# A hybrid MoBA/NSA decoder layer: k's norm weights applied behind the transposition, mixer B's gates finished in one piece, and a pair's first doubling put behind its subtraction

## The chip, the cores and the metric

The kernel runs on one core of a Trainium2 chip. Its five engines are named as in the profile: PE (matrix products), DVE (vector), ACT (scalar), POOL (GpSimd) and SP (issues most DMAs). Each has its own stream of instructions and runs it in order; they wait for each other through semaphores. The metric is the device time of one execution in microseconds (us), as a median of several runs.

## The reference

One decoder layer on x of 1 x 512 x 1024, all in float32. One input projection feeds two attention mixers of 8 heads with 64 channels each; their outputs are gated, projected, merged and projected once more. Cut to what the change touches:

```
h = rms_norm(x, norm_w);  proj = h @ w_in
q_a, k_a, v_a, z_a, q_b, kc, vc, ksl, vsl, kwn, vwn, gate_b, z_b, gate_m = split(proj)
o_a = moba_mixer(rms_norm(q_a, q_norm_a), rms_norm(k_a, k_norm_a), v_a, bias_a)
k_cmp = rms_norm(compress(kc), k_norm_cmp);  v_cmp = compress(vc)
o_b = nsa_mixer(rms_norm(q_b, q_norm_b), k_cmp, v_cmp,
                rms_norm(ksl, k_norm_sel), vsl, rms_norm(kwn, k_norm_win), vwn, gate_b, bias_b)
# in nsa_mixer: g = sigmoid(gate_b);  o = g0 * o_cmp + g1 * o_sel + g2 * o_win
y = sigmoid(gate_m) * (o_a*silu(z_a) @ w_branch_a) + ... (o_b*silu(z_b) @ w_branch_b)
x = x + y @ w_out
```

`rms_norm(k, g)` divides each head's 64 values by their root mean square and multiplies them by the 64 weights g. These weights are the same for all tokens. Since q and k only meet in the product q.k, the kernel multiplies the weights of q into those of k, with the factor 1/8 of the logits, and never touches q with them.

## The kernel before

**Products.** Each float32 product is made as three products of high and low parts (`mm3`, L386): a value is rounded to fp32r (its high part, a CAST) and the rest is a second fp32r tile (its low part, a subtraction). For weights, `wh` is made by ACT (L352), or now and then by POOL (L356) or DVE, and `wl = wr - wh` by DVE (L361, also for `vl`), now and then by POOL.

**Projections by token.** `proj_norm` runs over four tiles of 128 tokens for `qk0` and `qk1` (mixer A: four heads of q and four of k in 512 columns each) and for `kb` (mixer B: two groups of k_sel and of k_win, 256 columns, and 24 gate columns behind them). PE accumulates a tile into PSUM (`pgt`). Then `norm` (L709) makes a chain of steps: ACT copies the tile with the token's factor (L718) and squares it (L720), DVE sums per head (L721), DVE and POOL make the factors `nr` (L426, L427), DVE or POOL multiplies (L723). The last step multiplies k by its weights: for `qk` the second half of the columns (L726, 128x256, eight of them), for `kb` all columns (L729, 128x256, four of them). `gi` says which weights: 1 for mixer A's k, 4 and 5 for k_sel and k_win, 0 for none.

**Gates of mixer B.** With each tile of `kb`, ACT writes exp(-x) of the 24 gate columns into `ge` (L745), and at the end of the chain DVE adds 1 (L749) and writes the reciprocals into `gate[:, :, t]` (L750). `gate` is a 128x96 tile, read much later, when POOL scales the exponentials of mixer B's heads (L1062).

**Pairs of heads.** `k_pair` (L969) makes the k operands of two heads. PE transposes four 128x128 pieces into a PSUM bank (`pq`, L947, pool of three banks "t"). From its halves r = 0, 1 (64 partitions each) ACT writes the high part twice, into the lower and upper 64 partitions of `ks` (L978: four copies of 64x512 a pair), DVE subtracts to make the low part `kx` (L980, two a pair; the second frees the bank), and ACT doubles `kx` into its own upper 64 partitions (L983, two a pair). So a pair's chain is four copies, two subtractions, two doublings. PE's scores are `ks` by `qs` (L1024) and `kx` by `qs` (L1025), into `sps`. There are six pairs: four of mixer A and two of mixer B; the latter two also copy their first 128 columns into `kf` (L987).

**Around them.** `compress` makes mixer B's compressed keys: X differences and `xs` (L838, L706, L707), products `hps` (L862), `hs` (L868), their transposition `pu` (L873), then a chain of ACT and DVE on `gt` (L878 to L882), of which L882 frees the bank of `pu`. The softmax of a block of scores is DVE's L1043 (add the bias, take the row's maximum), ACT's L1058 (exponential and sum), DVE's L1061 (reciprocal), POOL's L1062 (scale); then PE transposes (`pt`, L1071), ACT and DVE split it into `ph` (L1083) and `pl` (L1085), and PE multiplies by v (`O`, L1105). `vb` (L768, L769) is mixer B's v.

**What sets the order.** A planner in Python runs while the program is built. Steps are put into a `Chain` with a cost for each engine that may do them (`c.do({"A": 478}, ...)`); a heap always takes the chain with the smallest time, gives its step to the engine on which the costs end it first, and advances that engine's planned time. PE's work is a set of generators that yield their costs. The order in which the planner emits is the order in which each engine runs. A step keeps its planned cost even if its function emits nothing.

**Constants.** `load_consts` (L1547) loads the constants tile `cst` in two parts (the identity first, the rest by the DMA at its end) and the gains `gn`, 6 x 64 numbers repeated on all partitions. DVE multiplies q's weights and 1/8 into k's (L1560, four products of 128x64).

## Time and profile before

| what | value |
|---|---|
| median of 3 runs | 452.53 us (452.14 to 452.53) |
| the profiled execution | 451.59 us |
| its span in the trace | 449.8 us |
| instructions | 8544 |
| clock granted to PE | 1.0 of full speed throughout |
| HBM traffic | 282 GB/s over the span |

Busy times are sums over the span and say nothing on where an engine is late. They are read by stretches, and together with PE's waits. A row of the timeline gives the start in us, the length in us, the engine, the line, the operation, what it writes and reads, shape and type, and how many such instructions follow each other; in brackets stands how long the engine stood idle before it, and what released it. A PE matmul's rows overlap: PE's rate is read from one start to the next. For instance, DVE's and ACT's groups with the most busy time are the low and high parts of the weights:

```profile
L361 DVE TENSOR_TENSOR wl<-wr,wh 128x512 fp32r<-128x512 f32 (+1 forms) x150 | 102.6, 701 | 2.1 <-ACT wh L352 1.8
L352 ACT CAST wh<-wr 128x512 fp32r<-128x512 f32 (+1 forms) x130 | 77.0, 608 | 15.3 <-DMA wr<-wsum 6.5
```

### The profile page before, as it was taken

The numbers are of one execution on the slowest core, as the hardware profiler recorded it, in microseconds if no ns is written. First come the engines' busy times: TensorE is split into PE (matmuls) and PEld (weight loads), VectorE is DVE, ScalarE is ACT, GpSimd is POOL, SyncE is SP. The second block draws the span as 40 slices with busy tenths as digits, with TensorE's granted clock in tenths as the row PEclk, the third lists the DMA queues.
The fourth block names the chain that finished last, engine by engine and source line by source line (L and its number), as shares of the span: only waits on it lengthen the run. The fifth ranks groups of instructions, "written<-read, shape, count | busy, mean of one in ns | idle before, by whom it ended". The sixth has DMA issues, their size and how long they took to land.

```text
span 449.8 us, 8544 instructions
## 1 busy us (share of the span) xinstructions
PE 441.8 (98%) x2779; PEld 394.0 (88%) x2779; DVE 384.0 (85%) x943; ACT 302.9 (67%) x711; POOL 198.9 (44%) x235
## 2 busy tenths in 40 slices
PE   8999999999999999999999999999999999999997
PEld 7878888899778899888999998989988999998886
DVE  5999899899998797788899899977967699899783
ACT  6866778867978798376878677687764355454450
POOL 1153337865675573177675654764850222211000
PEclk9999999999999999999999999999999999999999
DMA  8975746887975879858978876986767878789872
GB/s 262 305 253 187 242 150 213 196 228 187 267 181 165 214 220 270 290 142 202 287 213 204 228 181 170 253 218 156 213 166 174 256 220 253 223 245 290 278 237 95
DMA packets 55086, 98.21 MB, mean 218 GB/s; under 512 B 5313, under 2 KB 9537, under 8 KB 55041
## 3 DMA queue, kind: packets, MB, share of 16 engines
q1 hardware_dynamic: 39808, 68.30, 47.2%
q0 software_dynamic: 7616, 14.68, 20.4%
q10 hardware_dynamic: 7616, 14.68, 9.7%
q8 instruction: 22, 0.36, 0.3%
q14 instruction: 24, 0.19, 0.1%
HBM read 90.69 MB, written 36.31 MB: 282 GB/s over the span
## 4 chain that ended last, share of the span: by engine, by line
PE 77%; DVE 12%; ACT 4%; issue 3%; DMA 2%; POOL 0%; SPq 0%; DVEq 0%; ACTq 0%
PE pgw L386 18%; PE pgt L386 14%; PE pbr L386 9%; PE po L386 9%; PE pgc L386 7%; PE O L1105 6%; PE pt L1071 5%; PE sps L1024 3%; PE sps L1025 3%; DVE wl L361 2%; DMA wr<-in_wgate 2%; DVE sb L1043 1%; DVE pl L1085 1%; DVE sq L490 1%; PE pq L947 1%
## 5 line engine op out<-in xcount | busy, mean ns | idle before, releaser
L361 DVE TENSOR_TENSOR wl<-wr,wh 128x512 fp32r<-128x512 f32 (+1 forms) x150 | 102.6, 701 | 2.1 <-ACT wh L352 1.8
L352 ACT CAST wh<-wr 128x512 fp32r<-128x512 f32 (+1 forms) x130 | 77.0, 608 | 15.3 <-DMA wr<-wsum 6.5
L356 POOL TENSOR_SCALAR wh<-wr 128x512 fp32r<-128x512 f32 (+1 forms) x39 | 31.6, 822 | 76.4 <-DVE wl L361 34.4
L1062 POOL TENSOR_SCALAR P<-P,sst,gate 128x512 f32<-128x512 f32 (+3 forms) x56 | 46.2, 828 | 40.0 <-DVE sst L1061 32.0
L1058 ACT ACTIVATE P<-sb,sst 128x512 f32<-128x512 f32 (+3 forms) x88 | 50.7, 577 | 17.5 <-DVE sst L1043 16.0
L1043 DVE CUSTOM_DVE_ANT_0 sb<-sps,T 128x512 f32<-128x512 f32 (+3 forms) x96 | 46.0, 483 | 14.0 <-PE sps L1025 13.5
L386 PE MATMUL pgt<-wh,hh 128*128 128x512 f32 (+2 forms) x160 | 56.6, 354 | 0.0
L386 PE MATMUL pgt<-wl,hh 128*128 128x512 f32 (+2 forms) x160 | 55.8, 349 | 0.8 <-DVE wl L361 0.8
L386 PE MATMUL pgt<-wh,hl 128*128 128x512 f32 (+2 forms) x160 | 55.7, 348 | 0.0
L386 PE MATMUL pgw<-th,wh 128*128 128x256 f32 x240 | 48.9, 281 | 0.3 <-DVE gm L1519 0.3
L1083 ACT CAST ph<-pt 128x512 fp32r<-128x512 f32 (+2 forms) x72 | 33.8, 476 | 19.8 <-PE pt L1071 18.5
L386 PE MATMUL pgw<-hh,wh 128*128 128x256 f32 x160 | 45.1, 282 | 0.5 <-ACT c L1460 0.5
L386 PE MATMUL pgw<-hl,wh 128*128 128x256 f32 x160 | 44.3, 277 | 0.0
L386 PE MATMUL pgw<-hh,wl 128*128 128x256 f32 x160 | 44.3, 277 | 0.0
L1071 PE MATMUL pt<-cst,P 128*128 128x128 f32 x232 | 40.7, 272 | 0.3 <-DVE pl L1085 0.3
L1085 DVE TENSOR_TENSOR pl<-pt,ph 128x512 fp32r<-128x512 f32 (+2 forms) x72 | 38.7, 549 | 1.8 <-ACT ph L1083 1.5
L386 PEld LDWEIGHTS pgw<-th,wh 128*128 128x128 f32 x240 | 39.4, 188 | 0.8 <-DVE gm L1519 0.5
L427 POOL TENSOR_TENSOR nr<-nss,mhalf 128x8 f32<-128x8 f32 (+1 forms) x16 | 26.4, 1650 | 22.5 <-DVE nss L426 19.3
L386 PEld LDWEIGHTS pgt<-wl,hh 128*128 128x128 f32 x160 | 30.0, 188 | 5.2 <-DVE wl L361 1.2
L386 PE MATMUL pgw<-th,wl 128*128 128x256 f32 x120 | 33.3, 277 | 0.0
L386 PEld LDWEIGHTS pgt<-wh,hh 128*128 128x128 f32 x160 | 30.1, 188 | 3.4 <-ACT nraw L718 0.2
L386 PEld LDWEIGHTS pgt<-wh,hl 128*128 128x128 f32 x160 | 30.1, 188 | 3.3
(271 smaller groups left out, 1289.4 us busy)
## 6 DMA issues: line engine op xcount, KB each, us to landing
wr<-wsum SPq DMA_DIRECT2D x56, 256.0 KB, 3.8
wr<-in_wtok SPq DMA_DIRECT2D x36, 256.0 KB, 4.8
wsum<-in_wgate ACTq DMA_DIRECT2D x16, 512.0 KB, 5.2
wsum<-wsum POOLq DMA_DIRECT2D x14, 512.0 KB, 7.6
wr<-in_wgate SPq DMA_DIRECT2D x24, 256.0 KB, 5.0
xsum<-th SPq DMA_DIRECT2D x16, 256.0 KB, 2.3
T<-rtab SPq DMA_DIRECT2D x16, 256.0 KB, 5.3
wr<-in_w SPq DMA_DIRECT2D x16, 256.0 KB, 4.3
```

The costliest lines, as they stand in the source:

```text
L352: e.copy(hi, raw)
L356: e.tensor_scalar(hi, raw, 1.0, 1.0, op0=ALU.mult, op1=ALU.mult)
L361: c.do({"D": cd(n)} if lead else either(n), lambda e, hi=hi, lo=lo, raw=raw: e.tensor_sub(lo, raw, hi.bitcast(F32))).mark((w, 1, i))
L386: nc.tensor.matmul(dst, sts[i][a], mvs[i][b], start=(start and i == a == b == 0), stop=(stop and i == n - 1 and b == 1), skip_group_check= ...
L427: c.do({"p": 430 + POWC * w}, lambda e: e.tensor_tensor(v(dst), v(ss), mhalf[:parts, :w], op=ALU.pow))
L1043: e.tensor_tensor_reduce(z["sb"][:, :L], sps[:, :L], T[:, S - L:], scale=-1.0, scalar=3e38, op0=ALU.add, op1=ALU.min, accum_out=st[:, 0, b ...
L1058: e.activation(pv(), z["sb"][:, :L], AF.Exp, bias=st[:, 0, b:b + 1], scale=-1.0, accum_out=st[:, 1, b:b + 1])
L1062: c.do({"P": 315 + 0.834 * L}, lambda e: e.tensor_scalar(pv(), pv(), st[:, 2, b:b + 1], g, op0=ALU.mult, op1=ALU.mult))
L1071: nc.tensor.transpose(pt[:, (b - kb) * P:(b - kb + 1) * P], u.p0 if u.p0 is not None and b == 0 else u.pb[:, POFF[b] + kb * P:POFF[b] + (k ...
L1083: e.copy(z["w"][0], pt[:, :w])
L1085: ch.do({"D": cd(w)}, lambda e: e.tensor_sub(z["w"][1], pt[:, :w], z["w"][0].bitcast(F32)), pt)
L1105: nc.tensor.matmul(O[0][:, S - n:], v.bitcast(F32) if kb == 3 else v, w, start=(u.first and kb == 0 and i == 0), stop=(u.last and kb == 3 ...
```

## The change

1. **k's weights behind the transposition.** `norm` no longer multiplies by the weights of k (L726, L729); the planner still counts the steps' costs, so that it gives the other work the same order. In `k_pair` a channel of k is a partition, so the weights are one column of factors, `gcol`: the four ACT copies become activations with that column as their scale, and the two subtractions become `pt * gcol - ks`, one DVE instruction each.
2. **Where the column comes from.** The six gains stand as six more columns in the second part of the constants (`cst` grows from 128x486 to 128x492). Three of the four products with q's weights (mixer A's k, k_sel, k_win) are made there, 128x1 each; the fourth (for the compressed k) stays as it was.
3. **The gates finished once.** ACT writes exp(-x) straight into `gate[:, :, t]`; the addition and the reciprocal are left out for the first three tiles and done for all 96 columns with the fourth.
4. **The first doubling.** The doubling of the pair's first `kx` gets a chain of its own, due 600 ns behind the planned end of its subtraction, instead of standing behind the second subtraction.

```diff
--- before.py
+++ after.py
@@ -29,7 +29,7 @@
 C32 = 32
 CMPH = 256
 COFF, NCST = {}, 0
-for _n, _w in (("ident", P), ("ii", DH), ("cmask", NT * C32), ("rowv", NT), ("hmask", 2), ("pos", 32), ("w2", 256)):
+for _n, _w in (("ident", P), ("ii", DH), ("cmask", NT * C32), ("rowv", NT), ("hmask", 2), ("gcol", 6), ("pos", 32), ("w2", 256)):
     COFF[_n] = (NCST, _w)
     NCST += _w
 POFF = [0, 128, 384, 768]
@@ -55,6 +55,7 @@
 LAND = 1000
 SLOW = dict(D=1.01, A=1.01, P=1.05)
 POWC = 180
+KX0 = 600
 CMARGIN = 1000
 UNITS = 4
 W1B = 2
@@ -414,6 +415,7 @@
         return cst[:, o:o + n]
 
     ident = cview("ident")
+    gcol = cview("gcol")
     ii = cview("ii")
     cmask = cview("cmask").rearrange("p (b c) -> p b c", b=NT)
     rowv = cview("rowv")
@@ -722,11 +724,9 @@
         rsqrt_mean(ch, lambda: b["r"], lambda: b["ss"], DH, H)
         ch.do(either(n), lambda e: e.tensor_mul(out, b["raw"], b["r"].unsqueeze(2).to_broadcast([P, H, DH])), lambda: b["t"])
         if gi == 1:
-            z = out[:, 4:]
-            ch.do(either(256), lambda e: e.tensor_mul(z, z, gn[:, 1, :].unsqueeze(1).to_broadcast([P, 4, DH])))
+            ch.do(either(256), lambda e: None)
         elif gi:
-            z = out.rearrange("p (a b) d -> p a b d", a=2)
-            ch.do(either(256), lambda e: e.tensor_mul(z, z, gn[:, gi:gi + 2, :].unsqueeze(2).to_broadcast([P, 2, 2, DH])))
+            ch.do(either(256), lambda e: None)
 
     def hl4(t):
         return t.rearrange("p (h s d) -> p h s d", s=2, d=DH)
@@ -741,13 +741,13 @@
             toks[name][t] = att(name, F32)
             ch = Chain(now[0] + 230)
             if name == "kb":
-                e_ = sp.tile([P, 24], F32, name=nm("ge"), tag="ge", bufs=4)
-                ch.do({"A": 164}, lambda e: e.activation(e_, ps[:, 256:280], AF.Exp, scale=nrx[:, t:t + 1]))
+                ch.do({"A": 164}, lambda e: e.activation(gate[:, :, t], ps[:, 256:280], AF.Exp, scale=nrx[:, t:t + 1]))
             norm(ch, toks[name][t], ps, t, 4 if name == "kb" else 8, gi)
             if name == "kb":
                 def g1(e):
-                    e.tensor_scalar_add(e_, e_, 1.0)
-                    e.reciprocal(gate[:, :, t], e_)
+                    if t == NT - 1:
+                        e.tensor_scalar_add(gate, gate, 1.0)
+                        e.reciprocal(gate, gate)
                 ch.do({"D": 300}, g1)
             ch.mark(f"{name}.{t}")
         yield from gemm_tok(name, emit, tags)
@@ -966,21 +966,28 @@
                  pt if r else None)
             box.append((z, c))
 
-    def k_pair(boxes, name, col, firsts=None):
+    def k_pair(boxes, name, col, gi, firsts=None):
 
         yield room("t")
         pt = turn(name, col)
         yield 4 * 109
         c = Chain(now[0] + 230)
         kk = [(att("ks"), att("kx")) for _ in range(2)]
+
+        def double():
+            nc.scalar.copy(kk[0][1][64:128, :], kk[0][1][0:64, :].bitcast(F32))
         for r, (ks, kx) in enumerate(kk):
             for i in range(2):
-                c.do({"A": 478}, lambda e, r=r, z=ks[64 * i:64 * i + 64, :]: e.copy(z, pt[64 * r:64 * r + 64, :]))
+                c.do({"A": 478}, lambda e, r=r, z=ks[64 * i:64 * i + 64, :]: e.activation(
+                    z, pt[64 * r:64 * r + 64, :], AF.Copy, scale=gcol[64 * r:64 * r + 64, gi:gi + 1]))
         for r, (ks, kx) in enumerate(kk):
-            c.do({"D": 602}, lambda e, r=r, ks=ks, kx=kx: e.tensor_sub(
-                kx[0:64, :], pt[64 * r:64 * r + 64, :], ks[0:64, :].bitcast(F32)), pt if r else None)
+            c.do({"D": 602}, lambda e, r=r, ks=ks, kx=kx: e.scalar_tensor_tensor(
+                kx[0:64, :], pt[64 * r:64 * r + 64, :], gcol[64 * r:64 * r + 64, gi:gi + 1], ks[0:64, :].bitcast(F32),
+                op0=ALU.mult, op1=ALU.subtract), pt if r else None)
+            if not r:
+                c.call(lambda: Chain(c.t + KX0).call(double))
         for r, (ks, kx) in enumerate(kk):
-            c.do({"A": ca(512)}, lambda e, kx=kx: e.copy(kx[64:128, :], kx[0:64, :].bitcast(F32)))
+            c.do({"A": ca(512)}, lambda e, r=r, kx=kx: r and e.copy(kx[64:128, :], kx[0:64, :].bitcast(F32)))
             for i, z in enumerate((ks, kx) if firsts else ()):
                 def f(e, dst=firsts[r][:, i, :], src=z[:, :P].bitcast(F32)):
                     if e is nc.scalar:
@@ -1166,7 +1173,7 @@
                 yield toks_of(f"v{h // 4}")
                 if h % 2 == 0:
                     yield from q_pair(qs, f"qk{h // 4}", h % 4 * DH)
-                    yield from k_pair(ks, f"qk{h // 4}", 256 + h % 4 * DH)
+                    yield from k_pair(ks, f"qk{h // 4}", 256 + h % 4 * DH, 1)
                 yield need("rtab")
                 yield room("T")
                 box["T"] = load_bias(h)
@@ -1187,7 +1194,7 @@
             if not g:
                 both.extend(att("kf").rearrange("p (i b c) -> p i b c", i=2, b=2) for _ in range(2))
                 for br in range(2):
-                    yield from k_pair(kbox, "kb", P * br, [z[:, :, br, :] for z in both])
+                    yield from k_pair(kbox, "kb", P * br, 4 + br, [z[:, :, br, :] for z in both])
             yield toks_of("qb")
             for i in range(2):
                 yield from q_pair(box["q"], "qb", 256 * g + P * i)
@@ -1557,8 +1564,9 @@
         t = dma(cst[:, P:], consts[:, P:], 2000)
         c = Chain(t)
         for i, k in ((0, 1), (2, 3), (2, 4), (2, 5)):
-            c.do({"D": 102}, lambda e, i=i, k=k: e.scalar_tensor_tensor(gn[:, k, :], gn[:, i, :], 0.125, gn[:, k, :], op0=ALU.mult,
-                                                                        op1=ALU.mult))
+            z = gn.rearrange("p k d -> p d k") if k == 3 else gcol.unsqueeze(1)
+            c.do({"D": 102}, lambda e, i=i, k=k, z=z: e.scalar_tensor_tensor(z[:, :, k], z[:, :, i], 0.125, z[:, :, k], op0=ALU.mult,
+                                                                             op1=ALU.mult))
 
     def gemms():
         yield from proj_v("v", ("v0", "v1"), True)
@@ -1804,7 +1812,7 @@
                     for j in range(8)])
     wo = f["w_out"][0].reshape(2, 4, P, 2, 512).transpose(3, 0, 1, 2, 4).reshape(4, 4, P, 512)
     onehot, cd = _consts()
-    cd.update(pos=posT.reshape(P, -1), w2=w2.reshape(P, -1))
+    cd.update(gcol=np.tile(gains.reshape(6, DH).T, (2, 1)), pos=posT.reshape(P, -1), w2=w2.reshape(P, -1))
     d = dict(x=f["x"][0], xT=f["x"][0].T[P:],
              x0=np.concatenate([f["norm_w"][0].reshape(KT, P).T, f["x"][0].T[:P]], 1), wtok=wtok, wchan=wchan, wz=wz, wgate=wgate, gains=gains, w1=w1,
              relone=np.tile(np.concatenate([np.tile(f["rel_bias"], 8), onehot], 1), (2, 1)), wbr=wbr, wout=wo,
```

The order of PE's and SP's instructions is the same as before, and POOL's too but for three rows that go. On DVE, rows go and none moves. Around the third tile of `kb`, DVE's order before was (`wl` low parts of weights, `kb` the normed tile, `gt` in the compression, `sb` and `sst` in the softmax, `ge` and `gate` the gates):

```order
L361 TENSOR_TENSOR wl_1725<-wr_1652,wh_1724 128x512
L729 TENSOR_TENSOR kb_1615<-kb_1615,gn 128x256
L882 SCALAR_TENSOR_TENSOR gt_1711<-gt_1711,pu_1707 128x128
L1043 ISA sb_1758,sst_1750<-sps_1745,T_1612 128x512
L1043 ISA sst_1750 128x1
L749 TENSOR_SCALAR ge_1616<-ge_1616 128x24
L750 RECIPROCAL gate<-ge_1616 128x24
L361 TENSOR_TENSOR wl_1713<-wr_1603,wh_1712 128x512
L1043 ISA sb_1775,sst_1750<-sps_1762,T_1612 128x384
```

DVE's order now, at the same place and on to the fourth tile's gates (line numbers are those of the changed kernel: L362 was L361, L1050 was L1043, L1092 was L1085, L1068 was L1061):

```order
L362 TENSOR_TENSOR wl_1707<-wr_1640,wh_1706 128x512
L882 SCALAR_TENSOR_TENSOR gt_1695<-gt_1695,pu_1691 128x128
L1050 ISA sb_1739,sst_1731<-sps_1726,T_1602 128x512
L1050 ISA sst_1731 128x1
L362 TENSOR_TENSOR wl_1697<-wr_1593,wh_1696 128x512
L1050 ISA sb_1754,sst_1731<-sps_1743,T_1602 128x384
L1050 ISA sst_1731 128x1
L1092 TENSOR_TENSOR pl_1748<-pt_1732,ph_1747 128x512
L1092 TENSOR_TENSOR pl_1763<-pt_1750,ph_1762 128x384
L1050 ISA sb_1772,sst_1731<-sps_1766,T_1602 128x256
L1050 ISA sst_1731 128x1
L1068 RECIPROCAL sst_1731<-sst_1731 128x1 x2
```
```order
L749 TENSOR_SCALAR gate<-gate 128x96
L750 RECIPROCAL gate<-gate 128x96
```

Three rows are gone between the first `wl` and the second, and one wider pair stands where the fourth pair of 24 columns stood. The doubling moves only in two pairs: by one row in the first, and by four in mixer B's first, whose place in ACT's order before was (`P` the exponentials, `vb` mixer B's v, `ph` a high part, `kf` first columns of k):

```order
L1058 ACTIVATE P_2246,sst_2255<-sb_2328,sst_2255 128x256
L768 ACTIVATE vb_2305<-pgt_2201,rx 128x2x64
L352 CAST wh_2360<-wr_1978 128x512
L768 ACTIVATE vb_2304<-pgt_2306,rx 128x2x64
L1083 CAST ph_2382<-pt_2370 128x256
L983 CAST kx_2228<-kx_2228 64x512
L768 ACTIVATE vb_2305<-pgt_2306,rx 128x2x64
```

ACT's order now (L1065 was L1058, L978 is the moved doubling, L353 was L352, L1090 was L1083):

```order
L1065 ACTIVATE P_2224,sst_2233<-sb_2306,sst_2233 128x256
L978 CAST kx_2206<-kx_2206 64x512
L768 ACTIVATE vb_2283<-pgt_2179,rx 128x2x64
L353 CAST wh_2338<-wr_1956 128x512
L768 ACTIVATE vb_2282<-pgt_2284,rx 128x2x64
L1090 CAST ph_2361<-pt_2349 128x256
L768 ACTIVATE vb_2283<-pgt_2284,rx 128x2x64
```

The doubling of the first `kx` has passed two `vb`, one `wh` and one `ph`; all else stands as it stood.

## The prediction

> **What bounds the kernel now.** I read the page's first part, then PE's waits, then busy time by stretch, and only then the timeline around the two waits that the change can reach.
>
> ```profile
> PE 441.8 (98%) x2779; PEld 394.0 (88%) x2779; DVE 384.0 (85%) x943; ACT 302.9 (67%) x711; POOL 198.9 (44%) x235
> ```
>
> PE is busy for 98% of the span, so work taken from DVE is worth something only where PE waits for DVE. PE's waits, with total, count and longest in us:
>
> ```profile
> PE sps L1025 <- ACT kx L983: 1.0, 1, 1.0
> ...
> PE pgt L386 <- DVE wl L361: 0.8, 1, 0.8
> ...
> PE prx L541 <- DVE dg L528: 0.4, 1, 0.4
> ...
> PE pu L873 <- DVE kx L980: 0.2, 1, 0.2
> ```
>
> Three of these lines are about the pairs' k or stand in the stretch of k's and the gates' work; prx is at the start. Busy time by stretch (columns: stretch, its length, busy us and instructions of PE, PEld, DVE, ACT, POOL, then clock, DMA share, GB/s):
>
> ```profile
> 31.00:100.00 69.00, 69.00 (x354) 58.52 (x353) 62.93 (x155) 51.38 (x116) 37.29 (x40) 1.00 0.67 199
> 100.30:125.80 25.50, 23.47 (x158) 20.59 (x156) 25.17 (x63) 20.66 (x51) 16.13 (x19) 1.00 0.85 226
> 126.20:155.00 28.80, 28.80 (x160) 24.15 (x159) 24.50 (x74) 23.50 (x57) 18.74 (x21) 1.00 0.67 184
> 155.10:174.40 19.30, 19.30 (x161) 19.03 (x160) 14.32 (x36) 18.84 (x45) 10.29 (x13) 1.00 0.85 228
> ```
>
> From 31 to 100 and from 126.2 to 155 PE never stands still: what DVE or ACT gain or lose there is covered by PE. From 100.3 to 125.8 DVE is the full engine (25.17 of 25.50) and PE the one that waits. From 155.1 to 174.4 ACT is the full one (18.84 of 19.30), with PE busy all along but for one wait at the end of it. The sum is therefore made in two places: **stretch 1**, which ends with PE's waits at 121.8 to 125.8, where less DVE work helps; **stretch 2**, which ends at 174.9, where more ACT work hurts.
>
> **What the edits cost by themselves.** Groups by form (busy us, mean ns of one, idle before):
>
> ```profile
> L978 ACT CAST ks<-pq 64x512 fp32r<-64x512 f32 x24 | 13.9, 580 | 0.4
> L718 ACT ACTIVATE nraw<-pgt,rx 128x512 f32<-128x512 f32 x12 | 8.2, 687 | 8.2 <-PE pgt L386 8.1
> L1083 ACT CAST ph<-pt 128x512 fp32r<-128x512 f32 x24 | 14.1, 585 | 17.3 <-PE pt L1071 17.1
> L980 DVE TENSOR_TENSOR kx<-pq,ks 64x512 fp32r<-64x512 f32 x12 | 8.2, 686 | 1.7 <-ACT ks L978 1.3
> L775 DVE SCALAR_TENSOR_TENSOR v<-pgf,rx,v 128x256 fp32r<-128x256 f32 x8 | 3.2, 470 | 0.0
> L1525 DVE TENSOR_TENSOR gm<-pgw,R 128x256 f32<-128x256 f32 x10 | 4.2, 418 | 0.0
> ```
>
> - ks copy with a column of factors: no such 64x512 form ran. The same engine reading 512 PSUM columns takes 585 as a plain CAST (L1083) and 687 with a column of factors (L718): +0.10 each. The bounds are 0 (half the partitions, or the extra hidden behind the instruction before) and +0.15. I take 0.10, from the nearest rows: 24 copies, 2.4 us on ACT, of which 3 lie in the full part of stretch 1 and 8 in stretch 2.
> - The subtraction with a factor: L775 against L1525 is 470 against 418 for 256 columns, +0.05 each, between 0 and +0.10; 12 of them, 4 in stretch 2.
> - The Trainium skill, "ScalarE: Activation LUTs", section What ACT_TABLE_LOAD costs, speaks against this edit: an ACTIVATE pays about 93 ns for each per-partition pointer operand that stands in place of an immediate. By it the 8 copies of stretch 2 would be 0.74 us; the trace agrees (687 against 585, 102 ns).
>
> The 8 multiplications on qk (L726) lie before 100, under PE's unbroken work: nothing. So does the doubling that moves by one row in the first pair.
>
> **The start.** Three of the four gain products become 128x1, and these three now wait for the second load of constants. Their row (shortest, median, longest in ns, first and last start):
>
> ```profile
> L1560 DVE SCALAR_TENSOR_TENSOR gn<-gn x4: 213/422/633, 18.3 to 23.1; 128x64 f32<-128x64 f32 x4
> ```
> ```profile
> 11.56 0.50 SPq L255 DMA_DIRECT2D cst<-in_consts  x1
> ```
> ```profile
> cst<-in_consts SPq DMA_DIRECT2D x1, 243.0 KB, 5.5
> ```
>
> The load lands at about 11.56 + 5.5 = 17.1 and the first product starts at 18.3 behind other work, so the new wait has over 1 us of room; without it, everything behind it on DVE (the squares, the low parts, dg) and the PE instruction prx would be late by what is missing. The longest products (0.63 against 0.21 for the same 64 columns) overlap POOL's splits, and a smaller one would be held beside them in the same way. I take 0; the gain is at most prx's 0.4.
>
> **Stretch 1.** DVE, from the wait at the top of the list to its end:
>
> ```profile
> 119.29 0.68 DVE L361 TENSOR_TENSOR wl<-wr,wh 128x512 fp32r<-128x512 f32 x1
> ...
> 122.76 0.42 DVE L729 TENSOR_TENSOR kb<-kb,gn 128x256 f32<-128x256 f32 x1
> 123.10 0.28 DVE L882 SCALAR_TENSOR_TENSOR gt<-gt,pu 128x128 f32<-128x128 f32 x1
> ...
> 123.91 0.53 DVE L749 TENSOR_SCALAR ge<-ge 128x24 f32<-128x24 f32 x1
> ...
> 124.69 1.07 DVE L361 TENSOR_TENSOR wl<-wr,wh 128x512 fp32r<-128x512 f32 x1
> ```
>
> L729, L749 and L750 go. POOL beside it:
>
> ```profile
> 123.79 0.61 POOL L723 TENSOR_TENSOR kb<-nraw,nr 128x256 f32<-128x256 f32 x1
> 124.48 0.73 POOL L729 TENSOR_TENSOR kb<-kb,gn 128x256 f32<-128x256 f32 x1
> ```
>
> L749 took 0.53 beside the one, L361 1.07 beside the other (0.68 at 119.29, alone). POOL's L729 goes too, so L361 loses its second brake. ACT and PE:
>
> ```profile
> 118.63 0.61 ACT L352 CAST wh<-wr 128x512 fp32r<-128x512 f32 x1
> ...
> 121.14 1.14 ACT L983 CAST kx<-kx 64x512 fp32r<-64x512 f32 x2
> 122.31 0.31 ACT L881 ACTIVATE gt<-gt 128x128 f32<-128x128 f32 x1
> ```
> ```profile
> 121.81 0.50 PE L1025 MATMUL sps<-kx,qs 128*128 128x512 f32 x1 [0.97 <-ACT kx L983]
> 122.15 0.60 PE L1071 MATMUL pt<-cst,P 128*128 128x128 f32 x4
> 122.50 0.42 PE L1024 MATMUL sps<-ks,qs 128*128 128x384 f32 x1
> ...
> 122.94 0.49 PE L1071 MATMUL pt<-cst,P 128*128 128x128 f32 x3
> 123.53 0.63 PE L947 MATMUL pq<-cst,qk 128*128 128x128 f32 x4
> ...
> 124.38 0.40 PE L386 MATMUL pgt<-wh,hh 128*128 128x512 f32 x1
> 124.62 0.40 PE L386 MATMUL pgt<-wh,hl 128*128 128x512 f32 x1
> 125.81 0.49 PE L386 MATMUL pgt<-wl,hh 128*128 128x512 f32 x1 [0.80 <-DVE wl L361]
> ```
>
> Step by step:
> 1. ACT is back to back up to the doublings and carries 3 scaled copies: everything from 118.63 on is 0.3 later. The doubling and with it PE's sps go from 121.81 to 122.11. Here the change costs 0.3.
> 2. DVE's removals before this point are not kept: the L361 at 119.29 needs ACT's wh, which ended at 118.63 + 0.61 = 119.24 and now ends at 119.54. DVE waits there; what it saved earlier is gone.
> 3. Behind that DVE loses the second gate pair and its L729, but L882 needs ACT's L881, which ends 0.3 later, at 122.92. So L882 starts at about 122.94, where 123.10 stood: 0.16 kept.
> 4. The third gate pair is gone (124.69 - 123.91 = 0.78 kept): L361 starts at about 123.83. POOL's L723 ends there at 124.30 (its start goes with DVE by 0.1). Before, L361 ended 0.55 behind the end of POOL's L729 (125.76 against 125.21); with L723 as the brake it ends at 124.85, and PE's matmul, which began 0.05 behind it, at 124.90.
> 5. PE itself: four transposes at 122.15 took 0.35, so the three at 122.94 would have let pq start at 123.20, not 123.53: 0.33 was a wait for the bank that L882 frees. The 0.3 of step 1 falls into that wait; PE then reaches the wl matmul at 124.62 + 0.24 (as from 124.38 to 124.62) - 0.03 = 124.83.
> 6. So the matmul of 125.81 starts at 124.90 or, with the slower subtraction ahead of it, 124.95: **a gain of 0.86**. Its end on the good side is 1.0 (PE's own arrival at 124.83); on the bad side 0.5, if POOL's L723 goes with ACT's 0.3 rather than with DVE.
>
> The Trainium skill, "SBUF — State Buffer", section SBUF: two separate sides, calls the port that DVE and GpSimd share a lock: a DVE instruction with two SBUF inputs waits for all of a GpSimd one that began first. The trace agrees (L361 1.07 against 0.68); by it removing POOL's L729 helps only as far as L723 is over, as in step 4.
>
> The one pair that is left covers 96 columns. Reciprocals rise from
>
> ```profile
> L750 DVE RECIPROCAL gate<-ge x4: 305/306/306, 116.3 to 127.9; 128x24 f32<-128x24 f32 x4
> ```
>
> by at most the ratio of columns, to 1.2; I estimate 0.8 to 0.9, with the addition some 0.5 more than the pair there now. It stands at 127.7, under PE's unbroken work of 126.2 to 155: 0. Without that cover it would be 0.5.
>
> **Stretch 2.**
>
> ```profile
> 155.15 0.69 ACT L718 ACTIVATE nraw<-pgt,rx 128x512 f32<-128x512 f32 x1 [1.22 <-PE pgt L386]
> ```
> ```profile
> 172.39 0.68 DVE L980 TENSOR_TENSOR kx<-pq,ks 64x512 fp32r<-64x512 f32 x1 [0.79 <-ACT ks L978]
> ```
> ```profile
> 174.92 0.63 PE L873 MATMUL pu<-cst,hs 128*128 128x64 f32 x4 [0.23 <-DVE kx L980]
> ```
>
> ACT starts when PE releases it and then hardly stops. Eight copies stand between: +0.8 at the last of them, which DVE's subtraction already waits for. The doubling that moves ahead of vb, wh and ph puts ph and what follows it on DVE later by a copy, and one P waits for that: some +0.2, of which part returns when ACT comes to the doubling's old place; I count 0.1. Two slower subtractions add 0.1 up to the second kx, which frees the bank that pu waits for. PE waits already, so all of it shows: **a loss of 1.0**, between 0.6 (copies +0.05, no effect of the order) and 1.5 (copies +0.15, the order 0.2).
>
> **Sum** against the profiled execution's 451.59: -0.86 + 1.0 = +0.14, 451.73. The median of the runs shown, 452.53, is 0.94 above that execution; the same sum on it is 452.67, and I say 452.7. About 0.2% (0.9 us) is what a measurement of this kernel tells from no change; both halves are about that large, and their sum is not.
>
> **Rivals.**
> - **The factor is free (faster).** If a copy of 64 partitions takes the factor at no cost, stretch 2 loses at most 0.2 and stretch 1 keeps all: PE's 1.0 at 125.81 and up to 0.33 at 123.53. For it: the copies are half as high as any row I have. Against it: a copy of 64 partitions (580) takes as long as one of 128 (585), so height does not count. It gives 452.53 - 1.1 = 451.4.
> - **The path of wl turns to ACT and POOL (slower).** If L882 or POOL's L723 goes later with ACT's 0.3 and more, L361's end at 125.76 hardly moves, while stretch 2 loses its 1.0 to 1.5. The place is PE's matmul at 125.81, the price the lost 0.86, and it decides once L361 ends later than 125.5. For it: ACT is back to back ahead of L881. Against it: the 0.78 of the third gate pair stand behind L881. It gives 452.53 + 1.3 = 453.8.
> - **The change does not do what it says.** The order shows the rows gone and the wide pair in; I leave it 0.02, without effect on the time.
>
> **How the numbers follow.** Forecast 0.56 (all of its range, 452.53 - 0.4 to 452.53 + 0.9, within 0.2%), free factor 0.23, turned path 0.19, nothing done 0.02: faster 0.23, within 0.2% 0.58, slower 0.19. The likeliest one's own range is 452.1 to 453.4. The range on record takes in both rivals' times, 451.3 to 453.9, for about 0.85; with less of them it would leave out over 2 in 10.
>
> **What would show it.** In the profile after: ks copies of about 680; PE's sps wait about 1.3 in place of 1.0; the wl wait near 0.1 in place of 0.8; the wait of pu at about 1.2 in place of 0.2; one pair of gate rows with 96 columns. It is wrong if ks stays at 580, if pu's wait does not grow, or if a wait of over 0.3 stands at a place that I called covered, before 100 or behind 126.

## The result and the profile after

| | before | after |
|---|---|---|
| median, us | 452.31 (6 runs, 451.18 to 452.53) | 455.19 (6 runs, 454.82 to 456.14) |
| ratio, 95% interval | | 1.0064 (1.0048 to 1.0080) |
| the profiled execution, us | 451.59 | 456.14 |
| its span, us | 449.8 | 454.4 |

The change makes the kernel 2.9 us slower. The forecast was 452.7, the range 451.3 to 453.9.

The profile after, first part of the page (engine, busy us, share of the span, instructions):

```profile
PE 446.7 (98%) x2779; PEld 396.5 (87%) x2779; DVE 379.9 (84%) x928; ACT 305.5 (67%) x711; POOL 197.3 (43%) x232
```

DVE lost 4 us of work, and ACT gained 2.6 (2.4 were expected). But PE, with as many instructions in the same order, is busy for 4.9 us longer. That is the line to stop at. PE's waits after (total us, times, longest):

```profile
PE sps L1032 <- ACT kx L978: 1.1, 1, 1.1
PE pu L873 <- DVE kx L984: 1.0, 1, 1.0
...
PE pgw L387 <- DVE gm L1526: 0.5, 1, 0.5
```

The waits on which the prediction rested went the way it said, though none has quite the expected size: no wait of PE for wl is left (0.1 expected), the one for `pu` is 1.0 in place of 0.2 (1.2 expected), and the one for `sps` 1.1 in place of 1.0 (1.3 expected). One wait behind 126 grew, where all was to be covered: the one for `gm`, 0.5 in place of 0.3. Groups by form, ACT's copies and DVE's subtractions:

```profile
L981 ACT ACTIVATE ks<-pq,cst 64x512 fp32r<-64x512 f32 x24 | 16.4, 684 | 0.4
L984 DVE SCALAR_TENSOR_TENSOR kx<-pq,cst,ks 64x512 fp32r<-64x512 f32 x12 | 9.0, 748 | 3.2 <-ACT ks L981 3.0
```

The copy takes 684 ns (580 before), the subtraction 748 (686 before). The single pair of gate rows, and what stands behind it on DVE:

```profile
128.12 0.19 DVE L749 TENSOR_SCALAR gate<-gate 128x96 f32<-128x96 f32 x1
128.35 0.75 DVE L750 RECIPROCAL gate<-gate 128x96 f32<-128x96 f32 x1
129.02 0.10 DVE L1068 RECIPROCAL sst<-sst 128x1 f32<-128x1 f32 x1
129.35 0.22 DVE L904 TENSOR_SCALAR kr<-pk 64x64 f32<-64x64 f32 x1 [0.22 <-PE pk L896]
```

The pair takes 0.94 against 0.47 for one of 24 columns, and DVE still waits for PE behind it: covered, as expected.

So where is the time? Since PE's order is unchanged, the two traces can be compared matmul by matmul. Busy time by stretch, from 200 to 270, where PE stands still in neither trace; before:

```profile
200.00:270.00 70.00, 70.00 (x538) 66.97 (x538) 64.65 (x181) 52.99 (x137) 43.52 (x50) 1.00 0.83 215
```

and after:

```profile
200.00:270.00 70.00, 70.00 (x527) 66.62 (x526) 62.82 (x173) 52.20 (x134) 42.92 (x50) 1.00 0.84 212
```

In the same 70 us, at the same clock (1.00) and without a pause, PE started 527 matmuls in place of 538. It is slower while it runs. The timeline shows it too, at any place where products of the normed input follow each other; PE before:

```profile
35.65 0.39 PE L386 MATMUL pgt<-wl,hh 128*128 128x512 f32 x1
35.87 0.39 PE L386 MATMUL pgt<-wh,hh 128*128 128x512 f32 x1
36.10 0.39 PE L386 MATMUL pgt<-wh,hl 128*128 128x512 f32 x1
36.33 0.39 PE L386 MATMUL pgt<-wl,hh 128*128 128x512 f32 x1
36.55 0.39 PE L386 MATMUL pgt<-wh,hh 128*128 128x512 f32 x1
```

and after:

```profile
35.68 0.39 PE L387 MATMUL pgt<-wh,hh 128*128 128x512 f32 x1
35.92 0.40 PE L387 MATMUL pgt<-wh,hl 128*128 128x512 f32 x1
36.15 0.39 PE L387 MATMUL pgt<-wl,hh 128*128 128x512 f32 x1
36.38 0.40 PE L387 MATMUL pgt<-wh,hh 128*128 128x512 f32 x1
36.62 0.39 PE L387 MATMUL pgt<-wh,hl 128*128 128x512 f32 x1
```

Four steps take 0.90 us before and 0.94 after. The column of lengths (0.39) hardly shows it: only the starts do.

Not all matmuls are slower. The table gives the mean time from one start to the next, called a step below, worked out from the traces (the shortest four fifths of each group, ns). Of the two names behind the arrow, the first is the operand that streams through PE, the second the one that is loaded as PE's weights; `th`, `yh` and `mh` are high parts of later values of the layer:

```
                         before    after
pgt<-wl,hh   512 cols     227.2    231.9
pgc<-hl,wh   512 cols     228.7    232.6
pgw<-hl,wh   256 cols     113.4    118.2
pgw<-th,wh   256 cols     113.9    114.3
pbr<-yh,wh   512 cols     230.2    229.7
po<-wh,mh    512 cols     226.8    226.9
```

The products with `hh` or `hl` (the normed input's high and low part) are 3 to 6.5 ns slower, and the products of the same kind without them moved by 1 at most. Only the 192 `pgt` of 256 and 280 columns, which use `hh` and `hl` too, moved by under 2 ns. There are 1200 products with `hh` or `hl`; matched one by one, those whose step differs by under 30 ns add up to 4.1 us. What sets `hh` and `hl` apart from all other operands is their place in memory: they are allocated ahead of `cst`, and the change makes `cst` 24 bytes a partition wider. From the built programs: `hh` stands at byte 2208 of a partition in both, and every operand behind `cst` stands 32 bytes further than before. The offset between `hh` and the weights has changed, and these traces show nothing else that has changed about these products.

### The profile page after: what moved, and what is told of

Read it like the earlier page. It is cut to its first block, busy times and chain, and to the rows that moved or that the text cites. A ratio compares the mean times of both kernels' runs of the same rounds, so it can differ in the third digit from the quotient of the medians.

```text
span 454.4 us, 8528 instructions
## 1 busy us (share of the span) xinstructions
PE 446.7 (98%) x2779; PEld 396.5 (87%) x2779; DVE 379.9 (84%) x928; ACT 305.5 (67%) x711; POOL 197.3 (43%) x232
## 4 chain that ended last, share of the span: by engine, by line
PE 79%; DVE 7%; ACT 7%; DMA 5%; issue 2%; SPq 0%; ACTq 0%; DVEq 0%
PE pgw L387 16%; PE pgt L387 14%; PE pbr L387 9%; PE po L387 8%; PE pgc L387 7%; PE O L1112 5%; PE pgf L677 5%; PE pt L1078 5%; PE sps L1032 3%; PE sps L1031 3%; DMA T<-rtab 2%; DMA wr<-in_wgate 2%; ACT ks L981 1%; DMA wr<-in_w 1%; DVE wl L362 1%
## 5 line engine op out<-in xcount | busy, mean ns | idle before, releaser
L362 DVE TENSOR_TENSOR wl<-wr,wh 128x512 fp32r<-128x512 f32 (+1 forms) x150 | 101.4, 693 | 2.4 <-ACT wh L353 1.9
L353 ACT CAST wh<-wr 128x512 fp32r<-128x512 f32 (+1 forms) x130 | 76.7, 608 | 16.5 <-DMA wr<-wsum 6.9
L357 POOL TENSOR_SCALAR wh<-wr 128x512 fp32r<-128x512 f32 (+1 forms) x39 | 30.3, 786 | 80.8 <-DVE wl L362 34.1
L1065 ACT ACTIVATE P<-sb,sst 128x512 f32<-128x512 f32 (+3 forms) x88 | 50.7, 577 | 16.6 <-DVE sst L1050 13.0
L1050 DVE CUSTOM_DVE_ANT_0 sb<-sps,T 128x512 f32<-128x512 f32 (+3 forms) x96 | 46.0, 483 | 16.3 <-PE sps L1032 13.7
L1090 ACT CAST ph<-pt 128x512 fp32r<-128x512 f32 (+2 forms) x72 | 33.8, 475 | 20.2 <-PE pt L1078 18.9
L1092 DVE TENSOR_TENSOR pl<-pt,ph 128x512 fp32r<-128x512 f32 (+2 forms) x72 | 38.7, 549 | 1.7 <-ACT ph L1090 1.5
```

What stands on the lines that cost most here:

```text
L353: e.copy(hi, raw)
L357: e.tensor_scalar(hi, raw, 1.0, 1.0, op0=ALU.mult, op1=ALU.mult)
L362: c.do({"D": cd(n)} if lead else either(n), lambda e, hi=hi, lo=lo, raw=raw: e.tensor_sub(lo, raw, hi.bitcast(F32))).mark((w, 1, i))
L1050: e.tensor_tensor_reduce(z["sb"][:, :L], sps[:, :L], T[:, S - L:], scale=-1.0, scalar=3e38, op0=ALU.add, op1=ALU.min, accum_out=st[:, 0, b ...
L1065: e.activation(pv(), z["sb"][:, :L], AF.Exp, bias=st[:, 0, b:b + 1], scale=-1.0, accum_out=st[:, 1, b:b + 1])
L1090: e.copy(z["w"][0], pt[:, :w])
```

## The experiments

Each is timed against the kernel before on the same chip; ratios are to it, with 95% intervals.

**Offsets.** Four kernels move tiles by means of an unused one and change nothing else. The edits, against the changed kernel, the kernel before (twice), and the changed kernel:

```diff
a1   cst = cp.tile([P, NCST], F32, name="cst")
+    cp.tile([P, 8], F32, name="spare8")
a2   cst = cp.tile([P, NCST], F32, name="cst")
+    cp.tile([P, 8], F32, name="spare8")
a3, a4
+    cp.tile([P, 8], F32, name="spare8")
     hh = cp.tile([P, KT, S], F32R, name="hh")
```

> The changed kernel with an unused tile of 32 bytes a partition behind cst: in the changed kernel cst takes 32 bytes more than before, so every tile behind it stands at 0 instead of 32 mod 64 bytes while hh and hl stay at 32; with the spare tile all stand at 32 again. Theory 1 (offset): the matmuls that read hh or hl with a weight tile, 4 to 5 ns slower each in the changed kernel, return to 227 ns for 512 columns and 113 for 256; time falls by 2.5 to 4 us to about 452.5. Rival (chip or run): the intervals have nothing to do with addresses; time stays at 455.2 and intervals at 231. Rival (the change's own waits): time falls by less than 0.5.

> The kernel before with the same spare tile of 32 bytes behind cst: hh and hl at 32, all behind at 0 mod 64, no other edit. Theory 1 (offset): 2.5 to 4 us slower, about 455 to 456, intervals of the hh and hl products 231 and 118. Rivals: no change, 452.3.

> The kernel before with the spare tile ahead of hh: hh, hl and all behind at 0 mod 64. Theory 1a (what counts is that the two operands differ by 32 mod 64): no change, 452.3, intervals 227. Theory 1b (what counts is that the weights stand at 0 mod 64): 2.5 to 4 us slower.

> The changed kernel with the spare tile ahead of hh: hh and hl at 0, weights and all else behind cst at 32 mod 64. Theory 1a (a difference of 32 between the operands costs): as slow as the changed kernel, 455.2. Theory 1b (weights at 0 cost): fast, about 452.5.

They left one puzzle (a1), so two larger distances followed, with spare tiles of 56 and of 24 numbers behind `cst` of the changed kernel:

> The changed kernel with an unused tile of 224 bytes a partition behind cst, so that all tiles behind it stand exactly 256 bytes further than before and keep their offset to hh and hl modulo 256. Theory 1 (offsets): all hh and hl products at 227 and 113 ns again, 452.8 (452.4 to 453.2): the change without its shift costs 0.35, which is 1.5 lost up to pu at 174.9 less 1.15 gained up to the wl matmul at 125.8. Rival (padding by 32 already gave all that offsets can give): 454.1 as with 32 bytes, pgw still 117 to 118.

> The same with 96 bytes: everything behind cst 128 bytes further than before. Theory 1a (the offset counts modulo 128): as c1_new_256, 452.8. Theory 1b (modulo 256 or more): part of the hh and hl products slow, up to 455.

What was measured, by how much the weights (and all behind them) moved against `hh`, in bytes; steps in ns as in the table above:

```
kernel           moved  median  ratio (interval)         pgt<-wl,hh pgc<-hl,wh pgw<-hl,wh pgw<-th,wh
before               0  452.3   1                             227.2      228.7      113.4      113.9
a3_old_shift         0  452.86  1.0004 (0.9990-1.0017)        227.1      228.7      113.7      114.1
c1_new_256         256  452.06  0.9999 (0.9988-1.0011)        227.2      228.8      113.5      113.9
after               32  455.19  1.0064 (1.0048-1.0080)        231.9      232.6      118.2      114.3
a2_old_pad          32  454.94  1.0046 (1.0027-1.0065)        232.2      232.8      118.2      114.3
a4_new_hhshift      32  455.44  1.0059 (1.0040-1.0077)        232.4      232.6      118.2      114.2
a1_new_pad          64  454.08  1.0033 (1.0017-1.0048)        230.1      232.5      118.2      113.9
c2_new_128         128  454.49  1.0062 (1.0037-1.0086)        230.9      231.3      115.4      114.8
```

The kernel before with 32 unused bytes (a2) is as slow as the changed one; the changed one with 224 unused bytes (c1) is as fast as the one before. So the loss is the shift, and the rest of the change is worth nothing that can be measured (0.9999, about 0.5 us either way; 452.8 had been expected of c1). a3 and a4 show that what counts is the distance to `hh`, not where the weights stand. My theory of a step of 64 bytes was wrong: at 64 and at 128 much of the loss stays, and only 0 and 256 are free of it. The count of PE in the stretch shows the same; a2:

```profile
200.00:270.00 70.00, 70.00 (x528) 66.75 (x527) 63.42 (x173) 52.33 (x137) 42.94 (x49) 1.00 0.80 212
```

and c1:

```profile
200.00:270.00 70.00, 70.00 (x538) 67.05 (x537) 64.49 (x180) 52.91 (x137) 43.14 (x50) 1.00 0.83 216
```

The distance between what, though? In all these kernels `th`, `yh` and `mh` moved along with the weights. The next kernel (on top of d2, below) moves the pool of the weights, with a few small tiles ahead of it, by 32 and all that stands behind it by 256:

```diff
     cst = cp.tile([P, NCST], F32, name="cst")
+    cp.tile([P, 8], F32, name="spare8")
...
             t = wp.tile([P, WT + 2 * SHIFT], F32R, name=nm(name), tag=f"{tag}{b}", bufs=1)
+            if side and b == NW - 1 and not spare:
+                spare.append(wp.tile([P, 56], F32, name="spare56", tag="spare", bufs=1))
```

> d2_gates_only with only the pool of the weights' halves 32 bytes further (a spare tile of 32 bytes ahead of it, one of 224 behind it, so that everything behind stands 256 further). So hh and hl stay, weights in the pool move by 32, and th, yh and mh, which never were slow so far, keep their offset to hh but not to the weights. Theory A (what counts is the offset between the two operands of one product): now pgw<-th,wh, pbr<-yh,wh and po<-wh,mh get slower too, 113.9 to about 118, 227 to about 231 for po, and pgt with weights from the pool as well; time 454.5 to 457. Theory B (what counts is where hh and hl stand against the rest): only products of hh and hl slow, th, yh and mh as before; 453.5 to 454.5. Rival C (neither): 451.

Measured: 455.19 us, 1.0054 (1.0034 to 1.0074). `po<-wh,mh` takes 233.4 ns a step (226.9 in d2), `pgw<-th,wh` 118.2 (113.8), `pgw<-hl,wh` 118.4 (113.6). Products without `hh` or `hl` are slow now as well, which rules out theory B: what counts is where the streaming tile and the weight tile stand to each other, as in theory A. But theory A isn't the whole rule. Half of the `pgt` of 512 columns take their `wh` and `wl` from the other pool, which moved by 256, so by theory A they should be at 227 and the other half at 232. In the built program the two halves alternate, three products of each in turn, and both take 230 ns on the mean (`pgt<-wh,hl` 228.0, `pgt<-wh,hh` 233.0). So a single step does not follow the distance of its own two operands alone; the operands of its neighbours, whose weights are loaded meanwhile, may count too. That was not separated.

**The parts of the change, on equal offsets.** The following are built on c1, except d2. c4 puts k's weights back ahead of the transposition, c5 only those of mixer B:

```diff
c4, in norm (gi 4 likewise) and in k_pair (the subtraction likewise)
-            ch.do(either(256), lambda e: None)
+            z = out[:, 4:]
+            ch.do(either(256), lambda e: e.tensor_mul(z, z, gn[:, 1, :].unsqueeze(1).to_broadcast([P, 4, DH])))
...
-                c.do({"A": 478}, lambda e, r=r, z=ks[64 * i:64 * i + 64, :]: e.activation(
-                    z, pt[64 * r:64 * r + 64, :], AF.Copy, scale=gcol[64 * r:64 * r + 64, gi:gi + 1]))
+                c.do({"A": 478}, lambda e, r=r, z=ks[64 * i:64 * i + 64, :]: e.copy(z, pt[64 * r:64 * r + 64, :]))
c5: the same where gi > 1
```

> c1_new_256 with k's weights multiplied in before the transposition again (plain copies and subtractions in the pairs, gains made as before); the gates finished once and the moved doubling stay. Theory (the factor on ACT's copies costs stretch 2): pu's wait falls from 1.0 to 0.3, the sps wait from 1.1 to 1.0; DVE's L729 come back and take 0.3 to 0.5 of the gain at the wl matmul. 451.9 (451.4 to 452.4). Rival (the doubling's place costs stretch 2): pu's wait stays at 0.7 or more, 452.8 or more.

> c1_new_256 with only mixer B's k_sel and k_win weighted before the transposition again; mixer A's pairs keep the factor. Theory: pu's wait 0.3 as in c4_weights_old, sps wait 1.1 to 1.3 as in the changed kernel (three copies of mixer A's pair stand there), gain at the wl matmul 0.3 to 0.6 less than in c1_new_256; 452.0 to 452.4. Rival (mixer A's copies cost elsewhere): slower than c4_weights_old by over 0.5.

c4: 451.34, 0.9977 (0.9961 to 0.9992). c5: 451.75, 0.9992 (0.9980 to 1.0005). Both are a little faster than expected. PE's wait for `pu` is 0.6 in both (0.2 before, 1.0 in c1), between the 0.3 of the theory and the 0.7 of its rival; c4:

```profile
175.62 0.63 PE L876 MATMUL pu<-cst,hs 128*128 128x64 f32 x4 [0.62 <-DVE kx L986]
```

With plain copies the moved doubling costs about 0.3 there (0.26 in d2, below, where it has its old place).

The doubling back in its old place (d1), the gates alone (d2), no weights at all (d3), and the gates tile by tile again (d4):

```diff
d1
-            if not r:
-                c.call(lambda: Chain(c.t + KX0).call(double))
...
-            c.do({"A": ca(512)}, lambda e, r=r, kx=kx: r and e.copy(kx[64:128, :], kx[0:64, :].bitcast(F32)))
+            c.do({"A": ca(512)}, lambda e, kx=kx: e.copy(kx[64:128, :], kx[0:64, :].bitcast(F32)))
d2, against the kernel before
-                e_ = sp.tile([P, 24], F32, name=nm("ge"), tag="ge", bufs=4)
-                ch.do({"A": 164}, lambda e: e.activation(e_, ps[:, 256:280], AF.Exp, scale=nrx[:, t:t + 1]))
+                ch.do({"A": 164}, lambda e: e.activation(gate[:, :, t], ps[:, 256:280], AF.Exp, scale=nrx[:, t:t + 1]))
...
-                    e.tensor_scalar_add(e_, e_, 1.0)
-                    e.reciprocal(gate[:, :, t], e_)
+                    if t == NT - 1:
+                        e.tensor_scalar_add(gate, gate, 1.0)
+                        e.reciprocal(gate, gate)
d4: d2's edit the other way round, with bufs=3
```

> c1_new_256 with the doubling of a pair's first kx in its old place; weights and gates as changed. Theory (of the 1.5 that stretch 2 loses, 1.2 are the factor on ACT's copies and 0.3 the doubling's new place): pu's wait about 0.7 in place of 1.0, 451.75 (451.4 to 452.1). Rival (the new place pays for itself): 452.1 or more, pu's wait 1.0 or more.

> The kernel before with the gates finished once and nothing else; no tile in front of the weights changes its size, so all offsets are those of before. Theory: the third pair of gate rows is what held the low part at 124.69; the wl matmul gains 1.0 to 1.2 as in c4_weights_old, and nothing is lost in stretch 2: 451.2 (450.8 to 451.6), the fastest of all. Rival (the multiplications L729 on DVE and POOL hold it as well): gain of 0.4 or less, 451.9.

> c1_new_256 with plain copies and subtractions in the pairs and no multiplication in the norm either: the k of mixer A, k_sel and k_win go without their norm weights, which leaves that part of the computation out. It prices the factor: against c1_new_256 only ACT's copies (683 to 580 ns) and DVE's subtractions (748 to 686) get shorter. Theory (the factor costs 1.0 to 1.2 in stretch 2, 0.2 in stretch 1): 450.9 (450.5 to 451.3), ks 580 ns, pu's wait 0.3 to 0.6. Rival (the factor is free there): 452.0.

> c1_new_256 with the gates finished tile by tile as before (three ge tiles in place of four, for room); weights and doubling as changed. Theory (the third gate pair is most of the gain in stretch 1): the wl wait returns to 0.4 to 0.7, time 452.6 (452.3 to 453.0). Rival (the gone L729 are most of the gain): the wl wait stays under 0.2, 452.1.

```
kernel           median  ratio (interval)         the edit undone or made alone
c1_new_256       452.06  0.9999 (0.9988-1.0011)   the whole change
d1_double_old    452.40  1.0004 (0.9988-1.0019)   without the doubling's new place
d4_gates_old     453.14  1.0016 (1.0004-1.0029)   without the gates in one piece
d3_no_weights    450.80  0.9968 (0.9951-0.9985)   without weights and factors
c4_weights_old   451.34  0.9977 (0.9961-0.9992)   weights as before
d2_gates_only    451.04  0.9969 (0.9956-0.9983)   the gates in one piece alone
```

These kernels ran on two chips, c1 and c4 on one and the others on another, so they are compared by their ratios. The gates in one piece are worth 0.8 us on top of the other parts (d4 against c1; their intervals just meet) and 1.4 alone (d2). The factor on ACT's copies and in the subtractions costs 1.4 (c1 against d3). The multiplications that it replaces are worth little: d2 keeps them and is as fast as d3, which has neither them nor the factor. The doubling's place makes no difference that can be told here (d1 against c1; PE's wait for `pu` is 1.0 in both), against what I expected. d2 is faster than both kernels, and it leaves the size of every tile ahead of the weights alone.

Rows of these traces show where. PE's wait for `pu` in c1:

```profile
175.03 0.63 PE L874 MATMUL pu<-cst,hs 128*128 128x64 f32 x4 [1.01 <-DVE kx L985]
```

and in d2:

```profile
174.12 0.63 PE L873 MATMUL pu<-cst,hs 128*128 128x64 f32 x4 [0.26 <-DVE kx L980]
```

The wl matmul with the gates tile by tile (d4):

```profile
125.53 0.50 PE L387 MATMUL pgt<-wl,hh 128*128 128x512 f32 x1 [0.33 <-DVE wl L362]
```

The wait of 0.8 before is 0.3 there with L729 gone and the gate pairs kept, a little under what was expected. It is none with both gone (c1), and none with the gates in one piece alone (d2). So at this matmul L729 is worth 0.5 while the gate pairs stand, and nothing once they are gone.

## Why the prediction was wrong

**The step that failed** is the one that reads "From 31 to 100 and from 126.2 to 155 PE never stands still: what DVE or ACT gain or lose there is covered by PE". It took PE's own rate as given, there and in all that lies behind 175, for which the sum has no term at all. The hh and hl products became slower in every stretch, and their 4.1 us spread as follows: 0.6 before 31, 1.2 from 31 to 100, 0.1 each in 100 to 126, 126 to 155 and 155 to 175, and 2.0 behind 175. So the term that the sum put at nothing without a reason is PE's own time. In the part on the start I priced the new columns of `cst` by when their load lands, and not by what moves behind them. The diff showed it (one more entry in the list that sizes `cst`), and the addresses in the built program would have.

In the two profiled executions the end moves by 4.4 us from c1 to the changed kernel: about these 4.1, and the longer wait for `gm` (0.5 against 0.2 in c1), besides smaller ones. The medians differ by 3.1, by the ratios 2.9. The profiled execution of the changed kernel is the slowest of its six, 0.95 above their median; what else makes up the difference is not shown.

**What the sum did claim** is tested by c1, which has all of the change but the shift. It forecast +0.14; c1 gives 0.9999 (0.9988 to 1.0011), no change. Its terms, read in c1's trace against the trace of before, matmul by matmul:

- *Stretch 1, 0.86 gained.* The wl matmul itself made up 0.96, and the product behind it 0.1. With what PE won back at `pq` and the scores just ahead of it (0.4) and what it lost behind the slower copies (0.3 from 120.2 to 121.8), it is 1.2. Step 4 had the mechanism the wrong way round: POOL's L723 was to start first and hold the low part. In the trace after, the low part started first and POOL's instruction (now L725) took 1.01 where it had taken 0.61; DVE:

```profile
125.50 0.69 DVE L362 TENSOR_TENSOR wl<-wr,wh 128x512 fp32r<-128x512 f32 x1
```

and POOL:

```profile
125.66 1.01 POOL L725 TENSOR_TENSOR kb<-nraw,nr 128x256 f32<-128x256 f32 x1
```

- So the low part ended at 126.19, and step 6's better end held; PE had no wait left at this matmul:

```profile
126.00 0.40 PE L387 MATMUL pgt<-wh,hh 128*128 128x512 f32 x1
126.23 0.40 PE L387 MATMUL pgt<-wh,hl 128*128 128x512 f32 x1
126.47 0.39 PE L387 MATMUL pgt<-wl,hh 128*128 128x512 f32 x1
```

- *Stretch 1, the 0.3 at sps.* PE's `sps` did start 0.3 later, measured from 119, but the wait itself grew by 0.1 only: PE came to it later as well.
- *Stretch 2, 1.0 lost.* Measured 1.5. The term of 1.0 was the second pair alone, and it gave 0.8 at `pu` and 0.1 just ahead of it; in the trace after, DVE's subtractions in front of it:

```profile
174.47 0.74 DVE L984 SCALAR_TENSOR_TENSOR kx<-pq,cst,ks 64x512 fp32r<-64x512 f32 x1 [0.90 <-ACT ks L981]
...
176.20 0.76 DVE L984 SCALAR_TENSOR_TENSOR kx<-pq,cst,ks 64x512 fp32r<-64x512 f32 x1
```

and PE behind them:

```profile
177.10 0.63 PE L873 MATMUL pu<-cst,hs 128*128 128x64 f32 x4 [1.01 <-DVE kx L984]
```

- Missed was that mixer B's first pair stops PE as well, in a stretch that I had called busy all along. PE's weight loads in c1 there:

```profile
163.61 0.20 PEld L1079 LDWEIGHTS pt<-cst,P 128*128 128x128 f32 x2 [0.31 <-PE pgt L387]
...
164.33 0.42 PEld L948 LDWEIGHTS pq<-cst,kb 128*128 128x128 f32 x4 [0.25 <-DVE kx L985]
```

- `pq` waits for the bank that the first pair's second subtraction frees, which ACT's copies made late; with the steps around it PE lost 0.65 between 161.8 and 165.9, of which 0.3 stand ahead of the `pt` transposes, and their cause was not looked for.
- *ACT's and DVE's prices*, 0.10 and 0.05 more an instruction, were 0.104 and 0.062. The Trainium skill, "ScalarE: Activation LUTs", section What ACT_TABLE_LOAD costs, gives about 93 ns for a pointer operand; the trace is near it, 684 against 580 ns on 64 partitions, 687 against 585 on 128.
- *The doubling's 0.1* is not seen while the copies carry the factor (d1), though with plain copies `pu` waits 0.6 with it and 0.3 without (c4 and d2).
- *The gates' last pair*, 0.5 more and covered: so it was. *The start*, 0: the three products took 0.15, 0.15 and 0.56 and the load was there in time.

Of the rivals, neither came true. The factor was not free (d3), and the path of wl did not turn to ACT and POOL (no wait for wl is left). What made the kernel slower was in none of my cases.

## What to carry to other kernels

When a change alters the size of any tile, compare the addresses of all operands before and after it, for PE above all: this kernel, bound by PE, lost more by 32 bytes than it won or lost by the work that was moved. Undo the shift with an unused tile before judging the rest. And where an instruction replaces another on the engine that is full in its stretch, look for every place where PE waits for that engine's chain, not only for the one with a wait in the trace of before.

## What the runs showed of the hardware that was not expected

- A float32r matmul of 512 columns took 227 ns or about 232 in these runs, one of 256 columns 113.5 or about 118, by where in a partition the tile that streams and the one that is loaded as weights stand to each other. Moving one of them by 256 bytes cost nothing, by 32 it cost most, by 64 and 128 it cost something for most groups. Both operands moved together change nothing (a3).
- The distance of the two operands modulo 256 does not by itself tell fast from slow. In the built program of the kernel before, the `pgw<-hh,wl` stand at 64 bytes and take 113 ns, the `pgt` of 256 columns stand at 64 as well, most of them, and take 118. In c2 the `pgw` stand at 64 and 192 again and take 115 to 116. So a shift has to be measured, and the rule behind it stays open.
- The trace shows no wait and no lower clock for it: PE is busy all the time and the clock reads 1.00. Only the steps from one start to the next show it, or the count of instructions in a stretch that has no pause.
- The Trainium skill, "SBUF — State Buffer", section SBUF: two separate sides, names the port pair of DVE and GpSimd as the only place of contention among the engines. These runs show that PE alone loses time by where its own operands stand. Whether it is the load of the next weights that meets the running stream, as the dependence on both operands suggests, or another part, was not tried; nor was a shift over 256, or why 64 spares the products of `pgt` in part and not those of `pgw`.
